# GpSimd's two-tensor operations in instructions of at most 256 columns

## The chip, the cores and the metric

The kernel runs on one core of a Trainium2 chip. Its engines take their instructions from queues of their own and meet at semaphores: TensorE (PE in the profile; PEld is its weight load), VectorE (DVE), ScalarE (ACT), GpSimd (POOL) and SyncE (SP), which here only issues transfers. The metric is the device time of one execution in microseconds, as the median of several runs.

## The reference

A decoder trunk of two layers over 16 + 1024 = 1040 tokens of width 1024, in float32. Layer 0 is a Mamba-2 mixer (SSD) with a convolutional gated FFN, layer 1 stick-breaking attention with the same FFN:

```python
h = concatenate([meta_tokens, x])
# layer 0
z, xbc, dt = split(rmsnorm(h) @ w_in); xbc = silu(dwconv4(xbc))
y = ssd(xbc, dt)                     # 32 heads of 64, 4 groups, state 128
h = h + (rmsnorm_by_group(y * silu(z)) * gate_g) @ w_out
h = h + ffn(rmsnorm(h))
# layer 1
k, v = split(rmsnorm(h) @ w_kv); q = rmsnorm(h) @ w_q
h = h + stick_breaking(q, k, v) @ w_o          # 16 heads of 64
h = h + ffn(rmsnorm(h))
out = rmsnorm(h)[16:]
# ffn(u): g, val = split(dwconv3(u @ w_up)); (silu(g) * val) @ w_down,  FF = 2816
```

## The kernel before

**Split operands.** Tokens lie along the free dimension in tiles of up to 348 columns, features in 128 partitions. A float32 operand of a matrix product is held as two tiles of type fp32r, a rounded part and the rest: ScalarE copies `w32` into `wh`, GpSimd (for most weights) or VectorE computes `wl = w32 - wh`, and `mm3` (lines 171 to 173) issues three matmuls, wh·uh, wh·ul and wl·uh. A weight tile has 1024 columns (768 or 512 in the output projections).

**Stages, in the order of time.** Read `x` and build the normed operands (to about 110 us); the SSD mixer (to 690), where `stream` runs the input projection's tiles between the chunks of 116 tokens; the output projection and the entry into the FFN (to 955); the up projection (to 1350); the down projection (to 1550); attention (to 2160); its output projection and the FFN's entry (to 2330); up (to 2740), down (to 2925) and the last norm.

**GpSimd's work on two tensors.** The rests of weights: `load_w` line 165 (with a scaling by a gain at line 162 for three uses), `up_weights` line 905 and `operands` line 1055, `weights` line 1114, and lines 1212 and 1217 for the first head pair. In the up projection also the sums and differences of halves of weight tiles, each 512 columns (lines 909 to 913). In the SSD stage, for every chunk: `ce` times the C matrix in `ssd_decays` (line 602; 8 heads by 116 columns), `xde` in `ssd_front` (line 631; 8 by 64) and the decayed `state` in `ssd_back` (line 650; 8 by 64). At the end a gain on 512 columns (line 1491). GpSimd also runs masks, memsets and sums of squares (`square_sum`, `parts` of the norm, line 321), which have at most 348 columns or are not touched.

**VectorE's work beside it.** The chunk's decays `dk` (line 598, eight instructions for a chunk), the gate norm (lines 209 to 212 and 545), splits into high and low parts (lines 190, 857, 1057), convolutions (line 296, one input in PSUM or in a copy `ft`), the gate product (line 947), sums of tiles in the up projection (line 955), the down projection's sums of operands (lines 1039 to 1050) and of products from PSUM (lines 403 and 1105).

**FFN.** Up and down use a seven-product scheme on halves of the operands. A block `b` of the up projection needs the weights f1 to f4, made by `up_weights` one block ahead: f1, f2 and f3 of 1024 columns, f4 of 512. The buffers `fh`/`fl` are two of each, `wh`/`wl` three. In the down projection every product takes an operand pair from `operands(i)`: differences on VectorE, `wh` and `gh` on ScalarE, `wl` on GpSimd, `gl` on VectorE.

**Order.** In the SSD stage and in attention (`manual_schedule`) PE, DVE, ACT and POOL run in the order of the code. Elsewhere the framework's planner orders each engine's instructions by its own estimate of costs when the program is built; a few edges (`behind`) pin single instructions. An instruction waits for the pieces of a tile that it reads, and engines serve their queues in order. GpSimd's queue also issues a few transfers (`spill`, line 382).

Of the kernel before, what the change touches and what calls it, by code (L numbers as in the profile page):

```python
# [8 lines left out]
F32 = mybir.dt.float32  # L9
F32R = mybir.dt.float32r  # L10
AF = mybir.ActivationFunctionType
ALU = mybir.AluOpType
# [57 lines left out]
ORD = ((0, 0), (1, 0), (0, 1), (1, 1), (0, 2), (1, 2))  # L70
XB, SQD = 9, (1, 4, 7)
SCALE = 0.125


_PAR = {}
_n = 0
for _name, _w in (
# [4 lines left out]
    _PAR[_name] = (_n, _w)  # L82
    _n += _w
NPAR = _n


class Trunk:
# [67 lines left out]
    def load_w(self, src, n, gain=None, out=None):  # L155
        nc = self.nc
        w32 = self.wp.tile([P, 1024], F32, tag="w32", name=self.nm("w32"))
        nc.sync.dma_start(w32[:, :n], src)
        if gain is not None:
            v = w32[:, :n].rearrange("p (k c) -> p k c", k=KD)  # L160
            g = gain.unsqueeze(2).to_broadcast([P, KD, n // KD])
            nc.gpsimd.tensor_tensor(v, v, g, op=ALU.mult)
        wh, wl = out or [self.wp.tile([P, 1024], F32R, tag=t, name=self.nm(t)) for t in ("wh", "wl")]
        nc.scalar.activation(wh[:, :n], w32[:, :n], AF.Copy)  # L164
        nc.gpsimd.tensor_tensor(wl[:, :n], w32[:, :n], wh[:, :n].bitcast(F32), op=ALU.subtract)  # L165
        return wh, wl

    def mm3(self, out, wh, wl, uh, ul, first, last, joins=False):
# [410 lines left out]
    def ssd_decays(self, g, ct, c, pool):  # L579

        nc = self.nc
        h0 = GH * g
        t0, n = CH[c]
        cc = 3 * (c % 3) + c // 3
        dk = pool.tile([P, 1024], F32, tag="D", name=self.nm("D"))
        dk = dk[:n, : GH * CB].rearrange("p (h l) -> p h l", h=GH)
        nc.sync.dma_start(dk, self.acs_d[c, h0 : h0 + GH].unsqueeze(0).to_broadcast([n, GH, CB]))
        dk = dk[:, :, :n]
        ce = None
        if c:  # L590
            ce = pool.tile([P, GH * CB], F32, tag="E", name=self.nm("E"), bufs=2)
            ce = ce.rearrange("p (h l) -> p h l", h=GH)
            nc.sync.dma_start(ce, self.ea_d[c, h0 : h0 + GH].unsqueeze(0).to_broadcast([P, GH, CB]))
            ce = ce[:, :, :n]
        yield dk, ce

        for i in range(GH):
            nc.vector.tensor_scalar(dk[:, i], dk[:, i], self.cols[:n, 1, cc, h0 + i : h0 + i + 1], 0.0, op0=ALU.subtract, op1=ALU.min)  # L598
        nc.scalar.activation(dk, dk, AF.Exp)
        yield  # L600
        if c:
            nc.gpsimd.tensor_tensor(ce, ce, ct[:, t0 : t0 + n].unsqueeze(1).to_broadcast([P, GH, n]), op=ALU.mult)
        yield

    def ssd_front(self, g, x, bt, ct, c, dk, pool):

        nc = self.nc
        h0 = GH * g
        tt = nc.vector.tensor_tensor
        t0, n = CH[c]  # L610
        cc = 3 * (c % 3) + c // 3
        e = t0 + n
        pcb = self.sm("cb")
        nc.tensor.matmul(pcb[:n, :n], bt[:, t0:e], ct[:, t0:e], start=True, stop=True)
        px = self.lg("px")
        for q in range(4):
            nc.tensor.transpose(px[:n, q * P : q * P + P], x[q][:, t0:e], self.ident)
        px = px[:n].rearrange("p (h d) -> p h d", h=GH)
        cbm = pool.tile([P, CB], F32, tag="cbm", name=self.nm("cbm"), bufs=2)
        tt(cbm[:n, :n], pcb[:n, :n], self.past[:n, :n], op=ALU.mult)  # L620
        xdt = pool.tile([P, GH, 64], F32, tag="xdt", name=self.nm("xdt"), bufs=2)
        tt(xdt[:n], px, self.cols[:n, 0, cc, h0 : h0 + GH].unsqueeze(2).to_broadcast([n, GH, 64]), op=ALU.mult)
        tt(dk, dk, cbm[:n, :n].unsqueeze(1).to_broadcast([n, GH, n]), op=ALU.mult)
        bk = xde = None
        if c < 8:
            pb = self.sm("pb")
            nc.tensor.transpose(pb[:n, :P], bt[:, t0:e], self.ident)
            bk = pool.tile([P, P], F32, tag="bk", name=self.nm("bk"), bufs=2)
            nc.scalar.activation(bk[:n], pb[:n, :P], AF.Copy)  # L629
            xde = pool.tile([P, GH, 64], F32, tag="xde", name=self.nm("xde"), bufs=2)  # L630
            nc.gpsimd.tensor_tensor(xde[:n], xdt[:n], self.cols[:n, 2, cc, h0 : h0 + GH].unsqueeze(2).to_broadcast([n, GH, 64]), op=ALU.mult)
        return xdt, xde, bk

    def ssd_back(self, g, x, c, dk, ce, xdt, xde, bk, state, pool):

        nc = self.nc
        h0 = GH * g
        t0, n = CH[c]
        cc = 3 * (c % 3) + c // 3
        e = t0 + n  # L640
        new = None
        if c < 8:
            ps = self.lg("S")
            nc.tensor.matmul(ps, bk[:n], xde[:n].rearrange("p h d -> p (h d)"), start=True, stop=True)
            new = pool.tile([P, GH, 64], F32, tag="state", name=self.nm("state"), bufs=2)
            psv = ps.rearrange("p (h d) -> p h d", h=GH)
            if c == 0:
                nc.scalar.activation(new, psv, AF.Copy)
            else:
                nc.gpsimd.tensor_tensor(new, state, self.cd[:, cc, h0 : h0 + GH].unsqueeze(2).to_broadcast([P, GH, 64]), op=ALU.mult)  # L650
                nc.vector.tensor_tensor(new, new, psv, op=ALU.add)
        py = self.sm("y")
        for i in range(GH):
            q, r = i // 2, 64 * (i % 2)
            y = py[r : r + 64, q * CB : q * CB + n]
            nc.tensor.matmul(y, xdt[:n, i, :], dk[:, i, :], start=True, stop=c == 0)
            if c:
                nc.tensor.matmul(y, state[:, i, :], ce[:, i, :], start=False, stop=True)
        for q in range(4):
            nc.vector.scalar_tensor_tensor(x[q][:, t0:e], x[q][:, t0:e], self.par("d_skip", 4 * g + q),  # L660
                                           py[:, q * CB : q * CB + n], op0=ALU.mult, op1=ALU.add)
        return new
# [227 lines left out]
    def up_weights(self, layer, b, pool):  # L890


        nc, a = self.nc, self.a
        H = D // 2
        tt = nc.gpsimd.tensor_tensor
        g, v = (self.wp.tile([P, 1024], F32, tag="w32", name=self.nm("w32")) for _ in range(2))
        nc.sync.dma_start(g, a["w_up"][layer, b])
        nc.sync.dma_start(v, a["w_up"][layer, KF + b])
        x, y = (pool.tile([P, QW], F32, tag="x32", name=self.nm("x32"), bufs=2) for _ in range(2))

        def parts(t, n, own):
            p, tags = (pool, ("fh", "fl")) if own else (self.wp, ("wh", "wl"))
            hi, lo = (p.tile([P, 1024], F32R, tag=tag, name=self.nm(tag)) for tag in tags)
            nc.scalar.activation(hi[:, :n], t, AF.Copy)  # L904
            tt(lo[:, :n], t, hi[:, :n].bitcast(F32), op=ALU.subtract)  # L905
            return hi, lo

        f1 = parts(g, D, False)
        tt(x[:, :H], v[:, :H], v[:, H:], op=ALU.add)
        tt(x[:, H:D], x[:, :H], g[:, :H], op=ALU.subtract)  # L910
        f2 = parts(x[:, :D], D, True)
        tt(y[:, :H], g[:, :H], v[:, :H], op=ALU.subtract)
        tt(y[:, H:D], g[:, H:], x[:, H:D], op=ALU.subtract)
        f3 = parts(y[:, :D], D, True)
        yield [(*f1, 0), (*f1, H), (*f2, H), (*f2, 0), (*f3, 0), (*f3, H)]
        f4 = parts(v[:, H:], H, False)
        yield [(*f4, 0)]
# [75 lines left out]
    def down(self, layer, gd, hd, pool, after, each=None):  # L993
# [4 lines left out]
        FN, S, H = FFN[layer].tile, FFN[layer].half, D // 2  # L998
        wide = FFN[layer].wide
        tt = nc.vector.tensor_tensor  # L1000
        pt = nc.gpsimd.tensor_tensor
        ADD, SUB = ALU.add, ALU.subtract
        half = lambda j: slice(S - S * j, 2 * S - S * j)

# [185 lines left out]
    def heads(self, u, p, pool):  # L1190
# [4 lines left out]
        class Pair:  # L1195
# [4 lines left out]
            def load(me, kind):  # L1200
# [8 lines left out]

                def scale():  # L1210
                    v = w32.rearrange("p (k c) -> p k c", k=KD)
                    nc.gpsimd.tensor_tensor(v, v, self.par(gain, 0, KD).unsqueeze(2).to_broadcast([P, KD, P]), op=ALU.mult)

                def parts():
                    me.w[kind] = wh, wl = [self.wp.tile([P, 1024], F32R, tag=t, name=self.nm(t)) for t in ("wh", "wl")]
                    nc.scalar.activation(wh, w32, AF.Copy)
                    nc.gpsimd.tensor_tensor(wl, w32, wh.bitcast(F32), op=ALU.subtract)

                def some(k0):

# [250 lines left out]
    def finish_tokens(self, h, chunks):  # L1471
# [10 lines left out]
        for i, (t0, m) in enumerate(chunks):  # L1482
            y = self.Q("y")[:, :D]
            for b in range(2):
# [3 lines left out]
                    nc.tensor.transpose(p[:m, k * P : k * P + P], h[4 * b + k][:, t0 : t0 + m], self.ident)  # L1488
                if b:
                    nc.scalar.activation(y[:m, w], p[:m], AF.Copy, scale=r[:m, i : i + 1])  # L1490
                    nc.gpsimd.tensor_tensor(y[:m, w], y[:m, w], self.gfin[:m, w], op=ALU.mult)
                else:
                    nc.vector.scalar_tensor_tensor(y[:m, w], p[:m], r[:m, i : i + 1], self.gfin[:m, w], op0=ALU.mult, op1=ALU.mult)
            nc.sync.dma_start(self.a["out"][t0 : t0 + m, :], y)
# [138 lines left out]
```

## Time and profile before

| | |
|---|---|
| runs shown, median (lowest to highest) | 2992.21 us (2991.93 to 2997.83) |
| profiled execution: time / span from first to last instruction | 2995.8 / 2994.1 us |
| mean granted TensorE clock | 0.983 |
| TENSOR_TENSOR instructions on GpSimd | 621 |

The profile is of one execution. Times in it are microseconds from the first instruction. A row of the timeline reads: start, duration, engine, line, operation, output<-inputs, shape, count, and in brackets how long the engine was idle before it and what ended that. A group row gives busy time and mean nanoseconds of one; a row of one line's instructions gives least, median and longest nanoseconds. "Busy" counts an instruction from its start to its end, waiting for a port included. Matmuls overlap, so their rows last longer than their distance.

### The profile page before, as it was taken

What the parts mean: (1) busy time and instruction counts of PE and PEld (TensorE: products, weight loads), DVE (VectorE), ACT (ScalarE), POOL (GpSimd) and SP (SyncE); (2) the same over time, 40 slices, a digit from 0 to 9 for tenths busy, and PEclk for the clock granted to TensorE, in tenths of its full rate; (3) what the DMA queues carried; (4) which work ended last, traced back from release to release, by engine and by line L of the source; (5) the groups of instructions that cost most, each with busy time, mean ns of one, the idle gap of its engine ahead of it and who ended that gap; (6) DMA issues with size and microseconds to landing.
All of it is one profiled execution on the core that took longest, in us unless ns stands there. A gap on an engine that the chain in (4) does not pass through costs nothing.

```text
span 2994.1 us, 57318 instructions
## 1 busy us (share of the span) xinstructions
PE 2879.0 (96%) x21863; PEld 2738.0 (91%) x21863; DVE 2304.0 (77%) x4026; ACT 1653.4 (55%) x3403; POOL 1308.0 (44%) x1250
## 2 busy tenths in 40 slices
PE   7999999989998999999999999999899999999998
PEld 4999898879998999998999999999798999998878
DVE  5586868885369887878876888888839878878785
ACT  4555555553245555555334788887736555554433
POOL 1254444442334666663442222222342766764451
PEclk9999999999999999999999999999999999999999
DMA  5233333323122222224232122221331222225321
GB/s 162 70 107 90 106 89 105 106 70 139 63 80 72 79 73 84 79 86 177 74 130 86 55 61 66 64 70 54 106 141 57 80 84 78 75 82 176 106 99 64
DMA packets 123411, 272.72 MB, mean 91 GB/s; under 512 B 13664, under 2 KB 53216, under 8 KB 123136
## 3 DMA queue, kind: packets, MB, share of 16 engines
q1 hardware_dynamic: 117760, 257.93, 26.6%
q10 hardware_dynamic: 4112, 6.56, 0.7%
q0 software_dynamic: 1264, 4.57, 0.4%
q8 instruction: 172, 2.82, 0.4%
q14 instruction: 103, 0.84, 0.1%
HBM read 200.89 MB, written 53.20 MB: 85 GB/s over the span
## 4 chain that ended last, share of the span: by engine, by line
PE 77%; DVE 12%; issue 4%; ACT 3%; POOL 2%; DMA 2%; SPq 0%; DVEq 0%; ACTq 0%; POOLq 0%
PE p L172 9%; PE p L171 9%; PE p L173 9%; PE acc L172 6%; PE acc L171 6%; PE acc L173 6%; PE pj L171 6%; PE pj L172 6%; PE pj L173 6%; PE po L1366 3%; PE lg L1325 3%; PE wT L1352 2%; DVE D L598 1%; PE ms L831 1%; DVE xbc L545 1%
## 5 line engine op out<-in xcount | busy, mean ns | idle before, releaser
L171 PE MATMUL pj<-uh,wh 128*128 128x348 f32 (+2 forms) x1536 | 507.0, 330 | 11.7 <-ACT bk L629 5.9
L172 PE MATMUL pj<-ul,wh 128*128 128x348 f32 (+2 forms) x1536 | 499.7, 325 | 0.0
L173 PE MATMUL pj<-uh,wl 128*128 128x348 f32 (+2 forms) x1536 | 496.3, 323 | 0.0
L171 PE MATMUL p<-bh,fh 128*128 128x262 f32 (+1 forms) x1408 | 403.5, 287 | 7.7 <-ACT c L293 2.8
L173 PE MATMUL p<-bh,fl 128*128 128x262 f32 (+1 forms) x1408 | 402.6, 286 | 3.6 <-POOL fl L905 3.6
L172 PE MATMUL p<-bl,fh 128*128 128x262 f32 (+1 forms) x1408 | 402.3, 286 | 0.1
L905 POOL TENSOR_TENSOR fl<-x,fh 128x1024 fp32r<-128x1024 f32 x88 | 212.4, 2414 | 267.4 <-ACT fh L904 217.7
L172 PE MATMUL p<-bl,wh 128*128 128x262 f32 (+1 forms) x1056 | 302.0, 286 | 6.1 <-DVE bl L857 6.1
L171 PEld LDWEIGHTS pj<-uh,wh 128*128 128x128 f32 x1536 | 292.8, 191 | 16.2 <-ACT xbc L293 4.3
L171 PE MATMUL p<-bh,wh 128*128 128x262 f32 (+1 forms) x1056 | 302.8, 287 | 0.9 <-ACT bh L856 0.9
L173 PE MATMUL p<-bh,wl 128*128 128x262 f32 (+1 forms) x1056 | 301.9, 286 | 0.0
L165 POOL TENSOR_TENSOR wl<-w,wh 128x1024 fp32r<-128x1024 f32 (+2 forms) x76 | 155.7, 2050 | 318.7 <-ACT wh L164 318.7
L172 PEld LDWEIGHTS pj<-ul,wh 128*128 128x128 f32 x1536 | 293.2, 191 | 1.8 <-issue 1.0
L173 PEld LDWEIGHTS pj<-uh,wl 128*128 128x128 f32 x1536 | 292.7, 191 | 0.8 <-issue 0.8
L296 DVE SCALAR_TENSOR_TENSOR c<-p,params,c 128x260 f32<-128x260 f32 (+1 forms) x528 | 249.8, 481 | 54.6 <-ACT c L293 45.1
L171 PEld LDWEIGHTS p<-bh,fh 128*128 128x128 f32 x1408 | 270.2, 192 | 8.6 <-ACT c L293 6.0
L173 PEld LDWEIGHTS p<-bh,fl 128*128 128x128 f32 x1408 | 269.4, 192 | 4.1 <-POOL fl L905 4.0
L172 PEld LDWEIGHTS p<-bl,fh 128*128 128x128 f32 x1408 | 270.2, 192 | 0.6 <-DVE bl L857 0.5
L947 DVE TENSOR_TENSOR c<-c,c 128x260 f32<-128x260 f32 (+1 forms) x176 | 245.0, 1394 | 5.5 <-ACT c L943 2.4
L952 ACT ACTIVATE ft<-p 128x262 f32<-128x262 f32 (+1 forms) x352 | 127.4, 384 | 203.8 <-DVE p L955 177.0
L1055 POOL TENSOR_TENSOR wl<-w,wh 128x1024 fp32r<-128x1024 f32 x56 | 148.9, 2662 | 205.4 <-ACT wh L1054 195.7
L171 PE MATMUL acc<-gh,wh 128*128 128x260 f32 (+1 forms) x672 | 215.0, 323 | 10.9 <-DVE h L1105 7.2
(325 smaller groups left out, 8472.7 us busy)
## 6 DMA issues: line engine op xcount, KB each, us to landing
w<-in_w_up SPq DMA_DIRECT2D x88, 512.0 KB
w<-in_w_down SPq DMA_DIRECT2D x44, 512.0 KB
w<-in_w_in SPq DMA_DIRECT2D x40, 512.0 KB
E<-ea_d SPq DMA_DIRECT2D x32, 464.0 KB
D<-acs_d SPq DMA_DIRECT2D x32, 420.5 KB
g<-c SPq DMA_DIRECT2D x88, 130.0 KB
g<-c SPq DMA_DIRECT2D x88, 128.0 KB
b<-g SPq DMA_DIRECT2D x16, 520.0 KB
```

The source lines that it names most:

```text
L165: nc.gpsimd.tensor_tensor(wl[:, :n], w32[:, :n], wh[:, :n].bitcast(F32), op=ALU.subtract)
L171: mm(out, wh, uh, start=first, stop=False, skip_group_check=joins)
L172: mm(out, wh, ul, start=False, stop=False, skip_group_check=joins)
L173: mm(out, wl, uh, start=False, stop=last, skip_group_check=joins)
L296: nc.vector.scalar_tensor_tensor(out, ps[:, o + i : o + i + n], wcol(i), out, op0=ALU.mult, op1=ALU.add)
L905: tt(lo[:, :n], t, hi[:, :n].bitcast(F32), op=ALU.subtract)
L947: self.last_up = tt(g[:, :FN], g[:, :FN], v[:, :FN], op=ALU.mult)
L952: nc.scalar.activation(s[:, :N], ps[:, :N], AF.Copy)
L1055: pt(wl, y, wh.bitcast(F32), op=SUB)
L1325: nc.tensor.matmul(ps[:nt, :m], part[:, c0 : c0 + nt], ks[a][:, s0 : s0 + m], start=x == 0, stop=x == 1)
L1352: nc.tensor.transpose(pt[:ns, x * CB : x * CB + nt], bt[a][:nt, x * CB : x * CB + ns], self.ident[:nt, :nt])
L1366: nc.tensor.matmul(po[64 * a : 64 * a + 64, :nt], v[: CH[c][1], c, 64 * a : 64 * a + 64], wt[a][: CH[c][1], c, :nt], start=x == 0, stop=x ...
```

## The change

Every `tensor_tensor` of GpSimd with more than 256 columns is issued as several instructions, each over at most 256 columns (for three-dimensional operands as many whole rows of the first free dimension as fit: two of 116 or 128 columns, four of 64). A new function does it, and the calls go through it. Operands, results and the order of the calls stay as they are; the other engines' code is not touched.

```diff
+PIECE = 256
...
+def pieces(eng, out, x, y, op):
+
+    n = out.shape[1]
+    size = 1
+    for d in out.shape[2:]:
+        size *= d
+    step = max(1, PIECE // size)
+    for a in range(0, n, step):
+        c = slice(a, min(a + step, n))
+        eng.tensor_tensor(out[:, c], x[:, c], y[:, c], op=op)
...
-        nc.gpsimd.tensor_tensor(wl[:, :n], w32[:, :n], wh[:, :n].bitcast(F32), op=ALU.subtract)
+        pieces(nc.gpsimd, wl[:, :n], w32[:, :n], wh[:, :n].bitcast(F32), ALU.subtract)
...
-            nc.gpsimd.tensor_tensor(ce, ce, ct[:, t0 : t0 + n].unsqueeze(1).to_broadcast([P, GH, n]), op=ALU.mult)
+            pieces(nc.gpsimd, ce, ce, ct[:, t0 : t0 + n].unsqueeze(1).to_broadcast([P, GH, n]), ALU.mult)
...
-                nc.gpsimd.tensor_tensor(new, state, self.cd[:, cc, h0 : h0 + GH].unsqueeze(2).to_broadcast([P, GH, 64]), op=ALU.mult)
+                pieces(nc.gpsimd, new, state, self.cd[:, cc, h0 : h0 + GH].unsqueeze(2).to_broadcast([P, GH, 64]), ALU.mult)
...
-        tt = nc.gpsimd.tensor_tensor
+        tt = lambda out, x, y, op: pieces(nc.gpsimd, out, x, y, op)
...
-        pt = nc.gpsimd.tensor_tensor
+        pt = lambda out, x, y, op: pieces(nc.gpsimd, out, x, y, op)
```

The same replacement is made for the scaling in `load_w`, for `xde`, at lines 1212, 1217 and 1491. Below the new function a line of the changed kernel has a number higher by 13.

More of the change, by code (lines that the diff above doesn't have):

```diff
@@ L161, in load_w @@
             g = gain.unsqueeze(2).to_broadcast([P, KD, n // KD])
-            nc.gpsimd.tensor_tensor(v, v, g, op=ALU.mult)
+            pieces(nc.gpsimd, v, v, g, ALU.mult)
         wh, wl = out or [self.wp.tile([P, 1024], F32R, tag=t, name=self.nm(t)) for t in ("wh", "wl")]
         nc.scalar.activation(wh[:, :n], w32[:, :n], AF.Copy)
-        nc.gpsimd.tensor_tensor(wl[:, :n], w32[:, :n], wh[:, :n].bitcast(F32), op=ALU.subtract)
+        pieces(nc.gpsimd, wl[:, :n], w32[:, :n], wh[:, :n].bitcast(F32), ALU.subtract)
         return wh, wl
@@ L630, in ssd_front @@
             xde = pool.tile([P, GH, 64], F32, tag="xde", name=self.nm("xde"), bufs=2)
-            nc.gpsimd.tensor_tensor(xde[:n], xdt[:n], self.cols[:n, 2, cc, h0 : h0 + GH].unsqueeze(2).to_broadcast([n, GH, 64]), op=ALU.mult)
+            pieces(nc.gpsimd, xde[:n], xdt[:n], self.cols[:n, 2, cc, h0 : h0 + GH].unsqueeze(2).to_broadcast([n, GH, 64]), ALU.mult)
         return xdt, xde, bk
@@ L1211, in scale @@
                     v = w32.rearrange("p (k c) -> p k c", k=KD)
-                    nc.gpsimd.tensor_tensor(v, v, self.par(gain, 0, KD).unsqueeze(2).to_broadcast([P, KD, P]), op=ALU.mult)
+                    pieces(nc.gpsimd, v, v, self.par(gain, 0, KD).unsqueeze(2).to_broadcast([P, KD, P]), ALU.mult)
                 def parts():
@@ L1216, in parts @@
                     nc.scalar.activation(wh, w32, AF.Copy)
-                    nc.gpsimd.tensor_tensor(wl, w32, wh.bitcast(F32), op=ALU.subtract)
+                    pieces(nc.gpsimd, wl, w32, wh.bitcast(F32), ALU.subtract)
                 def some(k0):
@@ L1490, in finish_tokens @@
                     nc.scalar.activation(y[:m, w], p[:m], AF.Copy, scale=r[:m, i : i + 1])
-                    nc.gpsimd.tensor_tensor(y[:m, w], y[:m, w], self.gfin[:m, w], op=ALU.mult)
+                    pieces(nc.gpsimd, y[:m, w], y[:m, w], self.gfin[:m, w], ALU.mult)
                 else:
```

## The prediction

> **What bounds the kernel now.** First the page's busy shares and its chain of waits, then the table by stage (from and to, length, busy time of PE, PEld, DVE, ACT and POOL with instructions, granted clock, DMA), to see where TensorE is not fed.
>
> ```profile
> PE 2879.0 (96%) x21863; PEld 2738.0 (91%) x21863; DVE 2304.0 (77%) x4026; ACT 1653.4 (55%) x3403; POOL 1308.0 (44%) x1250
> ...
> PE 77%; DVE 12%; issue 4%; ACT 3%; POOL 2%; DMA 2%; SPq 0%; DVEq 0%; ACTq 0%; POOLq 0%
> ```
>
> ```profile
> 110.00:690.00 580.00, 552.01 (x3998) 515.22 (x3997) 443.04 (x910) 302.70 (x434) 256.10 (x137) 0.97 0.32 94
> ...
> 975.00:1350.00 375.00, 375.00 (x3081) 375.00 (x3081) 300.88 (x479) 217.69 (x439) 250.30 (x144) 1.00 0.25 83
> 1350.00:1570.00 220.00, 205.76 (x1684) 204.36 (x1683) 181.89 (x216) 90.05 (x127) 89.91 (x36) 0.98 0.36 124
> ...
> 2735.00:2930.00 195.00, 184.05 (x864) 151.97 (x863) 167.17 (x152) 76.36 (x93) 90.34 (x35) 0.97 0.30 104
> ```
>
> TensorE bounds it. In the up projection (975 to 1350) it is busy 375.00 of 375: nothing done to GpSimd or VectorE can win time there. What can be won lies in the joints between stages, where TensorE waits: 14.2 us in one down projection (220 - 205.76), 11.0 in the other, 28.0 in the SSD stage. So I asked the timeline for the waits of TensorE and for what stood before them.
>
> ```profile
> 843.92 0.39 PE L171 MATMUL acc<-y,w 128*128 128x260 f32 x1 [3.44 <-DVE h L403]
> 957.04 0.36 PE L171 MATMUL p<-bh,fh 128*128 128x262 f32 x1 [2.80 <-DVE c L296]
> 2332.47 0.36 PE L171 MATMUL p<-bh,fh 128*128 128x258 f32 x1 [2.83 <-ACT c L293]
> 1370.81 0.35 PE L171 MATMUL acc<-gh,wh 128*128 128x260 f32 x1 [1.36 <-DVE c L296]
> 1394.15 0.56 PE L171 MATMUL acc<-gh,wh 128*128 128x260 f32 x1 [4.95 <-DVE h L1105]
> 1484.00 0.39 PE L171 MATMUL acc<-gh,wh 128*128 128x260 f32 x1 [1.62 <-DVE h L1105]
> 1498.55 0.38 PE L171 MATMUL acc<-gh,wh 128*128 128x260 f32 x1 [2.31 <-DVE p L1105]
> 2758.39 0.80 PE L172 MATMUL acc<-gl,wh 128*128 128x512 f32 x1 [5.13 <-DVE gl L1057]
> 2890.00 0.50 PE L173 MATMUL acc<-gh,wl 128*128 128x512 f32 x1 [1.74 <-POOL wl L1055]
> ```
>
> Eight of these nine waits (24.4 us together) end on VectorE or on what follows it. Why VectorE is late, the following rows show:
>
> ```profile
> 943.78 2.41 POOL L905 TENSOR_TENSOR fl<-x,fh 128x1024 fp32r<-128x1024 f32 x1
> 943.85 2.63 DVE L955 TENSOR_TENSOR ft<-ft,ft 128x262 f32<-128x262 f32 x1
> 946.14 1.49 POOL L905 TENSOR_TENSOR wl<-w,wh 128x512 fp32r<-128x512 f32 x1
> 947.15 0.76 DVE L296 SCALAR_TENSOR_TENSOR c<-ft,params,c 128x260 f32<-128x260 f32 x1 [0.68 <-ACT c L293]
> 947.59 1.47 POOL L909 TENSOR_TENSOR x<-w 128x512 f32<-128x512 f32 x1
> 947.84 1.51 DVE L955 TENSOR_TENSOR ft<-ft,ft 128x262 f32<-128x262 f32 x1
> ```
>
> ```profile
> L947 DVE TENSOR_TENSOR c<-c,c x176: 411/1350/2601, 932.5 to 2742.2; 128x260 f32<-128x260 f32 x88, 128x256 f32<-128x256 f32 x88
> L1057 DVE TENSOR_TENSOR gl<-b,gh x56: 1209/1234/3446, 1351.5 to 2875.7; 128x1040 fp32r<-128x1040 f32 x28, 128x1024 fp32r<-128x1024 f32 x28
> ```
>
> L947 takes 0.41 us alone and 1.35 in the median: a VectorE instruction whose two inputs lie in SBUF runs only when GpSimd's two-tensor instruction has ended. L955 of 943.85 ends at 946.48, 0.3 after L905 (946.19). And the two take turns: GpSimd's next instruction is already issued at 946.14, yet VectorE comes in between, and GpSimd's takes 1.49 where its kind needs 1.29. So at each end of a GpSimd instruction the waiting VectorE instruction is let in, and no sooner.
>
> **The change part by part.** Nothing is computed otherwise; some 600 instructions become some 1,800.
>
> *What a piece costs.*
>
> ```profile
> 2945.11 1.54 POOL L245 TENSOR_TENSOR sq<-sq,sq 128x256 f32<-128x256 f32 x2 [17.41 <-ACT sq L239]
> 2949.47 0.73 POOL L245 TENSOR_TENSOR sq<-sq,sq 128x256 f32<-128x256 f32 x1 [2.81 <-ACT sq L239]
> ...
> 1066.62 2.39 POOL L905 TENSOR_TENSOR fl<-x,fh 128x1024 fp32r<-128x1024 f32 x1 [3.67 <-ACT fh L904]
> ...
> 1070.27 1.29 POOL L909 TENSOR_TENSOR x<-w 128x512 f32<-128x512 f32 x1
> ```
>
> 256 columns take 0.73 us. An instruction starts 0.04 before the one ahead ends (946.14 + 1.49 against 947.59, above), so pieces follow at 0.69: four take 3 x 0.69 + 0.73 = 2.80 against 2.39, +0.41 for 1024 columns; two take 1.42 against 1.29, +0.13 for 512. With about 255 of the first size, 32 of 928 columns priced like them and 310 of 512, GpSimd's own time grows by 287 x 0.41 + 310 x 0.13 = 158 us, to about 1,470. Bounds for a piece: 0.60 (a quarter of 2.39) and 0.73 plus the 0.08 that L245's pair of 1.54 shows between two dependent instructions, 0.81.
>
> The Trainium skill speaks against the change here: GPSIMD Engine Reference, section 2.1, says that every instruction is broadcast and then looked up in software, tens of cycles each. By that an estimate for 1,200 more instructions, at 50 cycles of its 1.2 GHz, is 50 us more of GpSimd's time; the row of 0.73 shows three times that, and the sum below would be the same by both, as long as the up projection hides it.
>
> *Up projection.* One block is 7 products of 12 matmuls for two tiles, 168 x 375/3081 = 20.4 us, with three instructions of 1024 (two `fl`, one `wl`) and five of 512 (`wl` of f4, L909, L910, L912, L913). They grow by 3 x 0.41 + 5 x 0.13 = 1.9, from 250.30/375 x 20.4 = 13.6 to 15.5. Let each of the ten VectorE instructions of a block that read two SBUF tensors (four L947, two L955, four L296 on `ft`) take its turn at 0.3, what is left of 0.41 once it is let in: 18.5. That still fits into 20.4, TensorE's time covers it: 0. If that cover is gone, each block is late by the excess.
>
> *VectorE's waits at the joints.* A blocked instruction now waits for one piece, 0.6 us at most for the part that holds it up, not up to 2.2.
>
> ```profile
> L190 DVE TENSOR_TENSOR y<-xbc,y x8: 687/1243/2831, 787.6 to 840.7; 128x520 fp32r<-128x520 f32 x8
> ```
>
> ```profile
> 835.54 2.42 DVE L190 TENSOR_TENSOR y<-xbc,y 128x520 fp32r<-128x520 f32 x2 [0.71 <-ACT y L189]
> ...
> 838.30 5.23 DVE L190 TENSOR_TENSOR y<-xbc,y 128x520 fp32r<-128x520 f32 x2
> ...
> 951.51 2.65 DVE L296 SCALAR_TENSOR_TENSOR c<-ft,params,c 128x260 f32<-128x260 f32 x1
> ...
> 2743.69 3.43 DVE L1040 TENSOR_TENSOR b<-b,b 128x1024 f32<-128x1024 f32 x1
> ```
>
> Before 843.92: a free L190 takes 0.69, a pair that follows at 0.6 some 1.30, so the second pair lost 3.93; at 0.6 each it loses 1.2. I take 2.7 of the 3.44. Before 957.04: L955 2.2, L955 1.1 and L296 2.17 lost, 5.5 in all, now 3 x 0.6: 3.7 saved, more than the wait; I take 2.4 of 2.80, and the same 2.4 for its twin at 2332.47. In the down projections long VectorE instructions of 1.23 stand in a row, and each piece left over blocks the next one, so most of the loss comes back in smaller parts: a 1024-column instruction that cost them 2.2 costs up to 4 x 0.6 = 2.4 while the row lasts. There I take 2.0 of 4.95 and 2.0 of 5.13 (bounds 0 and the whole), since the row ends in additions from PSUM (L1105) that wait for nobody. At 1370.81, 1484.00 and 1498.55 one blocked instruction stands just ahead of such an end: 1.0, 1.2 and 1.6. Together 15.3 us, between 5 and 24.4.
>
> *The clock.*
>
> ```profile
> 958.30:961.70 3.40, 3.40 (x18) 3.40 (x17) 3.28 (x7) 0.39 (x2) 0.75 (x1) 0.50 0.23 78
> 1391.80:1398.60 6.80, 4.45 (x20) 4.48 (x21) 6.80 (x9) 0.39 (x1) 0.79 (x1) 0.50 0.01 2
> ```
>
> Behind 957.04 the granted clock is 0.50 for 3.4 us, behind 1394.15 for 6.8; a wait that vanishes gives back half of that. I take 1.7 each for 957.04 and its twin, 3.4; none for the others (bounds 0 and 10).
>
> *First pieces.* At 2890.00 TensorE waits for a whole L1055; its first matmuls need the first 256 columns alone. I take 1.0 (bounds: -1.7 and +0.4, if it waits for all four).
>
> *What it costs.* In the SSD stage the order of GpSimd, VectorE, ScalarE and TensorE is that of the code, and 28 us of waits lie open.
>
> ```profile
> 337.78 0.63 PE L171 MATMUL pj<-uh,wh 128*128 128x352 f32 x1 [3.01 <-ACT bk L629]
> 298.93 1.60 DVE L598 TENSOR_SCALAR D<-D,cols 116x116 f32<-116x116 f32 x8
> ...
> 330.21 4.04 DVE L598 TENSOR_SCALAR D<-D,cols 116x116 f32<-116x116 f32 x8
> ...
> 329.62 2.21 POOL L602 TENSOR_TENSOR E<-E,xbc 128x928 f32<-128x928 f32 x1
> 331.77 1.05 POOL L650 TENSOR_TENSOR state<-state,cd 128x512 f32<-128x512 f32 x1
> ```
>
> Eight short L598 in a row are free at 298.93 (1.60) and meet L602 and L650 at 330.21 (4.04, so 2.4 lost). Every one of the five pieces still to come blocks the next of them, 5 x 0.6 = 3.0: +0.6. For some six such places, two at each end of a group: +3.6 (bounds -3 and +10, since single VectorE instructions ahead of them gain). L650's `new`, on which L651 waits, and L631's `xde`, on which L644 waits, come 0.15 later each, L602 and L165 0.41: VectorE is busy 443 of 580 here and takes most of it. With attention's first weights (L1212, L1217): +1.5.
>
> Sum: -15.3 - 3.4 - 1.0 + 3.6 + 1.5 = -14.6 us. The profiled execution took 2995.8 (span 2994.1), 3.6 above the median of the runs; 2995.8 - 14.6 = 2981.2, on the runs' scale 2992.2 - 14.6 = 2977.6.
>
> **Rivals.** *GpSimd becomes the bound in the up projection (slower).* It decides from (20.4 - 3.0)/22 = 0.79 us a piece. At the upper bound 0.81 each of some 42 blocks is 0.4 late; at 0.85, 1.3, or +55 - 15: 3032. The 0.73 speaks against it; that it is the price of an addition in place, not of `fl`, speaks for it. Chance 0.07.
>
> *No turn between pieces (slower):* GpSimd's next piece goes ahead of the waiting VectorE. Then a blocked instruction loses 2.8, not 2.2, at about 14 open places: +8, and +4 in the SSD stage: 3004. The row at 946.14 speaks against it. The Trainium skill (SBUF — State Buffer, "Who interferes with whom") says that the pair of ports is held for a whole instruction and that issue order decides; it does not say who comes next. Chance 0.08.
>
> *GpSimd falls behind long VectorE rows (no change).* If each piece yields to an instruction of 1.23, a `wl` takes 4 x (0.6 + 1.2) = 7.2 us where a product lasts 5.8 (48 matmuls at 375/3081 = 0.12); TensorE then waits for GpSimd instead, 1.4 at some ten products, and the 14.6 is gone: 2992. So too if the planner's order outside the two hand-ordered stages comes out worse. Chance 0.20.
>
> *All waits of the table and their dips vanish:* 24.4 + 10 - 5: 2963. Chance 0.11.
>
> **How the numbers follow.** The forecast (2970 to 2985) has 0.54. A measurement here tells 0.2%, 6 us, from no change: faster 0.54 + 0.11 = 0.65, within 0.17, slower 0.18 (the two slower rivals and a part of the third). The range reaches from 2958 (past the last rival) to 3003, which leaves out the larger half of the slower ones.
>
> **What would show it.** Right: 256-column instructions at 0.70 to 0.75 us; L947's median under 0.8; the waits at 843.92, 957.04 and 2332.47 under 1.0 with a clock of 1.00 behind them; POOL busy above 1,450 with the up stages still at full TensorE. Wrong: L947 still at 1.3 (no turns), new TensorE waits for `wl` or `fl`, or waits in the SSD stage grown by more than 10.

## The result, and the profile after it

The changed kernel takes 2966.02 us (median of 4 runs, 2962.1 to 2966.99) beside 2992.07 (2991.28 to 2997.83) before: the ratio is 0.9905, 95% interval 0.9893 to 0.9917. That is 26.1 us less; 14.6 were forecast. The profiled execution took 2966.99, its span is 2965.3, mean clock 0.989.

Busy times, chain of waits and GpSimd's costliest group, from the page after; then the rows of one line's instructions (least/median/longest ns) for the gate product (L947, now L960) and the sum of two copies (L955, now L968); then the stage table for the same matmuls of the up projection and for the SSD stage:

```profile
PE 2870.4 (97%) x21863; PEld 2730.3 (92%) x21863; DVE 2139.3 (72%) x4026; ACT 1649.1 (56%) x3399; POOL 1614.5 (54%) x2434
...
PE 81%; DVE 9%; issue 3%; ACT 2%; POOL 2%; DMA 2%; SPq 0%; DVEq 0%; ACTq 0%; POOLq 0%
...
L97 POOL TENSOR_TENSOR wl<-w,wh 128x256 fp32r<-128x256 f32 x780 | 692.1, 917 | 459.0 <-ACT wh L177 294.2
```

```profile
L960 DVE TENSOR_TENSOR c<-c,c x176: 414/566/962, 920.3 to 2715.8; 128x260 f32<-128x260 f32 x88, 128x256 f32<-128x256 f32 x88
...
L968 DVE TENSOR_TENSOR ft<-ft,ft x88: 419/773/6500, 903.3 to 2707.0; 128x262 f32<-128x262 f32 x44, 128x258 f32<-128x258 f32 x44
```

```profile
961.60:1336.60 375.00, 375.00 (x3079) 375.00 (x3079) 254.88 (x480) 219.78 (x440) 303.25 (x399) 1.00 0.25 82
110.00:685.00 575.00, 547.26 (x3980) 509.37 (x3980) 433.16 (x909) 301.03 (x435) 304.01 (x397) 0.98 0.32 95
```

(Every piece is L97.) The gate product's median fell from 1.35 to 0.57 us and its longest from 2.60 to 0.96, VectorE is busy 165 us less, GpSimd 307 more, and the up projection still runs at full TensorE. But one line got worse: the longest L968 takes 6.50, where L955 never took more than 2.65. TensorE's waits after, at the joint of 116 and at those of the forecast (at 843.92, 1370.81, 1484.00 and 2890.00 none is left; those at 958.19 and 2323.83 are new):

```profile
112.42 0.40 PE L184 MATMUL pj<-uh,wh 128*128 128x352 f32 x1 [0.67 <-DVE xbc L309]
958.19 0.39 PE L184 MATMUL p<-bh,wh 128*128 128x262 f32 x1 [1.93 <-ACT ft L965]
1378.45 0.56 PE L184 MATMUL acc<-gh,wh 128*128 128x260 f32 x1 [5.27 <-DVE h L1118]
1478.26 0.39 PE L184 MATMUL acc<-gh,wh 128*128 128x260 f32 x1 [1.02 <-DVE p L1118]
2323.83 0.56 PE L184 MATMUL p<-bh,wh 128*128 128x258 f32 x1 [2.20 <-ACT ft L965]
2733.89 0.80 PE L185 MATMUL acc<-gl,wh 128*128 128x512 f32 x1 [3.69 <-DVE gl L1070]
```

To see where the time went, each matmul of one profile is paired with the same one of the other (by line and by order on its line); the table has the median shift of the starts (us, after less before) in a window of 30 us around a time of before, and what the stage ahead of it added. The last column is the forecast's step.

| up to (time before) | shift | of it here | forecast |
|---|---|---|---|
| 100: load, operands | -4.7 | -4.7 | none |
| 150: the joint at 116 | -9.5 | -4.8 | none |
| 690: SSD | -6.9 | +2.5 | +3.6 |
| 870: output projection, wait at 843.92 | -11.8 | -4.8 | -2.7 |
| 1000: entry into the FFN, 957.04 and its dip | -13.4 | -1.6 | -4.1 |
| 1345: up | -13.4 | 0.0 | 0 |
| 1560: down | -19.2 | -5.8 | -5.8 |
| 2100: attention | -20.1 | -0.9 | +1.5 |
| 2290: its output projection | -21.7 | -1.6 | none |
| 2400: entry, 2332.47 and its dip | -23.1 | -1.3 | -4.1 |
| 2730: up | -23.1 | 0.0 | 0 |
| end: down, last norm | -28.8 | -5.8 | -3.0 |

The profiled execution of before lies 3.7 above its median of 2992.07, that of after 1.0 above its own: -28.8 + 2.7 = -26.1, as the runs have it. A single stage of one profile scatters by some 3 us where a clock dip comes or stays away: two kernels that differ from before only ahead of 125 us stood 2.7 and 3.4 later at 870 than at 830.

### The profile page after: what moved, and what is told of

The parts are those of the page before. It is cut to its first block, busy times and chain, and to the rows that moved or that the text cites. A ratio compares the mean times of both kernels' runs of the same rounds, so it can differ in the third digit from the quotient of the medians.

```text
span 2965.3 us, 58614 instructions
## 1 busy us (share of the span) xinstructions
PE 2870.4 (97%) x21863; PEld 2730.3 (92%) x21863; DVE 2139.3 (72%) x4026; ACT 1649.1 (56%) x3399; POOL 1614.5 (54%) x2434
## 4 chain that ended last, share of the span: by engine, by line
PE 81%; DVE 9%; issue 3%; ACT 2%; POOL 2%; DMA 2%; SPq 0%; DVEq 0%; ACTq 0%; POOLq 0%
PE p L184 10%; PE p L185 10%; PE p L186 10%; PE acc L185 7%; PE acc L184 7%; PE acc L186 7%; PE pj L184 6%; PE pj L185 6%; PE pj L186 6%; PE po L1379 3%; PE lg L1338 2%; PE wT L1365 2%; POOL wl L97 1%; PE ms L844 1%; DVE D L611 1%
## 5 line engine op out<-in xcount | busy, mean ns | idle before, releaser
L97 POOL TENSOR_TENSOR wl<-w,wh 128x256 fp32r<-128x256 f32 x780 | 692.1, 917 | 459.0 <-ACT wh L177 294.2
L97 POOL TENSOR_TENSOR fl<-x,fh 128x256 fp32r<-128x256 f32 x352 | 260.8, 772 | 165.4 <-ACT fh L917 113.5
L965 ACT ACTIVATE ft<-p 128x262 f32<-128x262 f32 (+1 forms) x352 | 133.3, 382 | 180.3 <-DVE p L968 108.1
L185 PE MATMUL acc<-gl,wh 128*128 128x260 f32 (+1 forms) x672 | 216.1, 322 | 3.7 <-DVE gl L1070 3.7
L186 PE MATMUL acc<-gh,wl 128*128 128x260 f32 (+1 forms) x672 | 215.0, 321 | 0.0
```

What stands on the lines that cost most here:

```text
L97: eng.tensor_tensor(out[:, c], x[:, c], y[:, c], op=op)
L185: mm(out, wh, ul, start=False, stop=False, skip_group_check=joins)
L186: mm(out, wl, uh, start=False, stop=last, skip_group_check=joins)
L965: nc.scalar.activation(s[:, :N], ps[:, :N], AF.Copy)
```

## The experiments

The theories: **A**, the gain is VectorE's shorter waits at GpSimd's instruction ends; **B**, it is the planner's order, which came out anew; **C**, it is readers that start on the first piece of a result; and, once L968's 6.5 us were seen, **D**, pieces can also shut VectorE out. Ratios are to the kernel before on the same chip (its medians there: 2989.5 to 2993.9).

### B: SP's order (b_pin), and the order of the decays' path (b_dt)

The 4.8 us at 116 lie ahead of all FFN work. VectorE's copy of `rows` and SP's transfers, before, after:

```profile
104.48 0.51 DVE L467 COPY rows<-rows 96x348 f32<-96x348 f32 x1
...
91.89 11.67 SPq L158 DMA_DIRECT2D w<-in_w_in  x2
105.01 0.81 SPq L471 DMA_DIRECT2D acs_d<-rows  x2
...
108.91 0.42 SPq L471 DMA_DIRECT2D acs_d<-rows  x1
...
120.45 0.63 PE L171 MATMUL pj<-uh,wh 128*128 128x348 f32 x1 [4.03 <-DVE xbc L296]
```

```profile
99.90 0.52 DVE L480 COPY rows<-rows 96x348 f32<-96x348 f32 x1 [2.60 <-PE rows L478]
...
91.31 0.33 SPq L171 DMA_DIRECT2D w<-in_w_in  x1
100.44 1.29 SPq L484 DMA_DIRECT2D acs_d<-rows  x3
```

Two things differ. A weight load no longer stands ahead of `acs_d` on SP. And the planner has ordered the decays' path anew: the three transfers of `acs_d` leave in a row, the last of them 7 to 8 us earlier, where the copy and all else are 4.6 to 4.7 earlier only because of the load stage (its VectorE waits, below). No GpSimd instruction runs between 103.2 and 111.5 before. b_pin moves the load alone; b_dt changes when the decays' path is called, and the planner then moves the load too. Neither has a piece:

```diff
-        nc.sync.dma_start(w32[:, :n], src)
+        pin(self, nc.sync.dma_start(w32[:, :n], src))    # the 9th load: behind the last transfer of E
```

```diff
-                if n % 3 == 2:
+                if n % 2 == 1:
                     next(dt, None)
```

> The kernel before with one edit: the ninth weight load of the input projection keeps to its place in the code, behind the chunk's decay transfers on SP's queue, instead of ahead of the transfers of acs_d. The planner moved that load there by itself when the pieces came in. Theory A (all of the gain comes from VectorE's shorter waits for GpSimd): nothing changes, 2992 +- 1, and TensorE's wait of 4.0 at 116 us stays. Theory B (the 4.8 us won between 100 and 125 us are SP's order, which has nothing to do with the pieces): 2992.1 - 4.8 = 2987.3 (2986 to 2989), the wait at 116 under 1.5.

> The kernel before, no pieces; only the three steps of the decays' path (dt_path) are called after tiles 1, 3 and 5 of the first group and not after 2, 5 and 8. By that the planner puts the exponentials of cd, cols and ea of ScalarE next to each other and the transfers of acs_d ahead of the ninth weight load, as in the changed kernel. Theory B2 (the 4.8 us won between 100 and 150 us come from the order of the decays' path on ScalarE, VectorE and TensorE, which the planner chose anew, and not from the pieces): TensorE's wait of 4.0 at 116 us becomes less than 1.5, 2992 - 4.8 = 2987 (2985 to 2989). Theory A (shorter waits of VectorE win them): 2992 +- 1.

b_pin: 2991.31, ratio 0.9996 (0.9985 to 1.0008); the joint takes 0.9 more, not 4.8 less. SP had only waited there for what wasn't ready. b_dt: 2990.5, 0.9993 (0.9982 to 1.0003); the joint takes 4.5 less than before:

```profile
117.42 0.40 PE L184 MATMUL pj<-uh,wh 128*128 128x352 f32 x1 [1.78 <-DVE xbc L309]
```

So the place of the load is refuted as the cause, and the planner's order of the decays' path makes such 4.5 us in a profile with not one piece in the kernel. There 3.4 of them were lost again at 843.92; in the median of the runs 2.1 are left, with an interval that includes no change at all. The order is a side effect of the change: with pieces of 512 it came out as before up to 118 us, and nothing was won at 116.

The planner changed its order in other places too, and no run holds it there. Between 850 and 1400 us VectorE and ScalarE run in the order of before (TensorE moves some matmuls near 930 and 1371); there 4.4 us were won. Elsewhere, near 840, 1480 to 1550, 2317 and 2765 among others, single instructions changed places, and more did near 710 and from 2200 to 2280. So at these joints B is not excluded by an experiment; for A speak the shorter waits in VectorE's own rows.

### A and C: other sizes (p512, p128), the reverse order (rev), FFN alone (ffn_only)

```diff
-PIECE = 256
+PIECE = 512        # p512; 128 in p128
...
-    for a in range(0, n, step):
+    for a in reversed(range(0, n, step)):        # rev alone, with PIECE = 256
```

ffn_only uses `pieces` only in `up_weights`, `operands` and `weights`.

> PIECE = 512. SP's order at 100 us is then that of the kernel before. Theory A: only the instructions of 1024 and 928 columns are split, a blocked VectorE instruction waits for 1.3 at most and not for 2.4, so about half of the remaining gain of 26.1 - 4.8 = 21.3 us is seen: 2992 - 10 = 2982 (2978 to 2987); the longest gate product (c<-c,c, 2.60 before, 0.96 with 256) about 1.7. Theory B alone (the planner's order makes the whole gain): 2992 +- 2.

> PIECE = 128. From 1.25 and 0.694 us between the starts of pieces of 512 and 256 columns a piece of 128 takes 0.416. A block of the up projection has 44 of them, 18.3 us, and with ten turns of 0.3 21.3, where TensorE needs 20.4. Rival 'GpSimd becomes the bound': 0.9 late in each of some 42 blocks, +38 - 28 = 3002 (2990 to 3020), TensorE waits for fl or wl in the up stages. If GpSimd's turns hide in each other it stays under TensorE's time: 2960 to 2966, the longest gate product at about 0.8.

> The pieces in reverse order, last columns first: a reader of the first 256 columns waits for all pieces, and VectorE's turns stay as they are. Theory A: 2966 to 2970, only the 1 to 2 us at 2890 are lost. Theory C (readers that start on the first piece make most of the gain): 2980 or more.

> Pieces only in up_weights and in the down projection (operands, weights); weights of the input and output projections, the SSD stage, attention and the end as before. Theory A: the gain of the joints at 844, 957, 1371 to 1500, 2332, 2758 and 2890 stays, 3.8 + 0.8 + 5.8 + 2.5 + 2.6 + 2.8 = 18, less what the 3.1 us of the start are, and the 4.8 at 116 are missing too: 2992 - 17 = 2975 (2972 to 2979).

| | median us | ratio (95%) |
|---|---|---|
| rev | 2965.71 | 0.991 (0.9894 to 0.9925) |
| p512 | 2970.42 | 0.9927 (0.9911 to 0.9943) |
| ffn_only | 2973.92 | 0.9935 (0.9922 to 0.9948) |
| p128 | 3105.82 | 1.038 (1.0360 to 1.0399) |

rev is as fast as the change: C falls, first pieces are worth nothing that can be seen. ffn_only wins 18.7 of the 26.1, as A has it. p512 wins 22 of them, more than the 10 expected, without the 4.8 at 116. In the first down projection half the relief was as good as all of it (6.3 won against 5.8); from 2730 to the end it won 2.7 against 5.8, where kernels with pieces of 256 in the down projection range from 2.7 to 6.7. At 957 and 2332 it was better (3.8 and 3.6 won there, against 0.8 to 1.6 and 0.5 to 1.3 with 256; the smaller number is counted from 930 and from 2320). p128 is slower by 3.8%, far past its expectation. The stage table of its first up projection, what TensorE waits for (from 980 to 1380), and L968 in the whole kernel:

```profile
1000.00:1390.00 390.00, 359.55 (x2842) 356.44 (x2841) 290.12 (x440) 198.23 (x407) 330.74 (x755) 0.97 0.22 70
```

```profile
PE p L184 <- ACT ft L965: 26.6, 13, 3.4
PE p L184 <- DVE c L309: 5.9, 3, 3.7
```

```profile
L968 DVE TENSOR_TENSOR ft<-ft,ft x88: 411/548/7891, 932.2 to 2835.1; 128x262 f32<-128x262 f32 x44, 128x258 f32<-128x258 f32 x44
```

GpSimd is idle for 59 of 390 us and TensorE never waits for `wl` or `fl` there: not GpSimd's own time is the bound. TensorE waits for copies (L965) that need the buffers of an L968 which VectorE could not begin; 37 of the 88 waited through four pieces or more.

### D: who is shut out (up512, turns, p128_turns)

One such wait in the changed kernel, VectorE's rows and then GpSimd's:

```profile
950.00 1.01 DVE L309 SCALAR_TENSOR_TENSOR c<-p,params,c 128x260 f32<-128x260 f32 x2 [0.84 <-ACT c L306]
950.93 6.29 DVE L968 TENSOR_TENSOR ft<-ft,ft 128x262 f32<-128x262 f32 x1
```

```profile
949.98 2.81 POOL L97 TENSOR_TENSOR fl<-x,fh 128x256 fp32r<-128x256 f32 x4
952.77 1.42 POOL L97 TENSOR_TENSOR wl<-w,wh 128x256 fp32r<-128x256 f32 x2
954.15 1.41 POOL L97 TENSOR_TENSOR x<-w 128x256 f32<-128x256 f32 x2
955.53 1.41 POOL L97 TENSOR_TENSOR x<-x,w 128x256 f32<-128x256 f32 x2
960.85 1.43 POOL L97 TENSOR_TENSOR fl<-x,fh 128x256 fp32r<-128x256 f32 x2 [3.92 <-ACT fh L917]
```

L968 passes eight piece ends (951.4 to 956.3) without its turn and ends 0.29 after GpSimd ran dry at 956.94; TensorE's wait at 958.19 follows. Before, a VectorE instruction saw one whole GpSimd instruction go by at most. When this L968 came, GpSimd was in the twelfth piece since it had last let VectorE in; those that came after up to eleven got in at the next end. turns measures this by itself (no part of the trunk is computed, the output is zeros): m operations of VectorE on PSUM, then one sum from SBUF, beside GpSimd's pieces on end. up512 gives only `up_weights` pieces of 512:

```diff
-        tt = lambda out, x, y, op: pieces(nc.gpsimd, out, x, y, op)
+        tt = lambda out, x, y, op: pieces(nc.gpsimd, out, x, y, op, 512)
```

> No trunk: the output is zeros, the kernel measures turns alone. In each of 26 trials GpSimd runs 34 differences of 256 columns (56 of 128, 24 of 512) on end; VectorE first runs m operations with one input in PSUM, then one sum of 262 columns from SBUF. Theory D, counted in pieces: the sum waits for one piece at most where it comes before the 12th piece, and until GpSimd is done where it comes later, for each size (m above 18 for 256, above 10 for 128, above 32 for 512). Counted in time (8 us): m above 17 for each size. Theory A alone: one piece at most in every trial.

> The changed kernel, but up_weights in pieces of 512 columns. In the changed kernel two additions ft<-ft,ft (950.93 and 2316.37) waited 6.3 and 6.5 us while GpSimd ran eight more pieces, and the joints at 957 and 2332 gave back 0.8 and 0.5 where the kernel with 512 everywhere gave back 3.8 and 3.6. Theory D (after some twelve pieces of GpSimd on end without a turn of VectorE, VectorE isn't let in until GpSimd runs dry; twelve pieces of 512 don't come about here): no VectorE instruction waits longer than 1.6, both joints win 3 more, 2966 - 6 = 2960 (2957 to 2963). If the two waits were chance: 2966 +- 1.

VectorE in turns, the last trial let in and the first shut out, for 256, 128 and 512 columns:

```profile
146.80 0.98 DVE L42 TENSOR_TENSOR q<-q,r 128x262 f32<-128x262 f32 x1
...
171.69 13.57 DVE L42 TENSOR_TENSOR q<-q,r 128x262 f32<-128x262 f32 x1
...
333.93 0.61 DVE L42 TENSOR_TENSOR q<-q,r 128x262 f32<-128x262 f32 x1
...
358.75 15.72 DVE L42 TENSOR_TENSOR q<-q,r 128x262 f32<-128x262 f32 x1
...
551.75 1.54 DVE L42 TENSOR_TENSOR q<-q,r 128x262 f32<-128x262 f32 x1
...
583.81 12.88 DVE L42 TENSOR_TENSOR q<-q,r 128x262 f32<-128x262 f32 x1
```

The sum is let in while GpSimd's 14th piece runs (13th with 512) and shut out from the 15th (16th, 14th) on: with 256 and 512 until the trial's last piece is done, with 128 until 3 to 9 of the 56 pieces are left, after 20 to 37 piece ends. Counted in time these limits are 9, 6 and 16 us: pieces count, not time. That is theory D, with 13 or 14 in place of 12; a 1024-column instruction in four pieces reaches that number four times sooner. But one wait of the same run doesn't fit it, that of the four-column copy with which the first trial of 512 opens:

```profile
447.30 29.27 DVE L39 COPY d<-gone 128x4 f32<-128x4 f32 x1 [1.38 <-POOL gone L35]
```

It came while the trial's first piece ran, three pieces of the trial before behind VectorE's last turn, and waited through all 24; in the other trials this copy got in by the end of the first piece. GpSimd had not run dry between these two trials, as it had between the others.

up512: 2963.65, 0.9904 (0.9889 to 0.9918). Its longest L968 takes 1.6 us, and the two waits and dips are gone; stage rows of the changed kernel, then of up512, around 958:

```profile
955.00:962.00 7.00, 5.07 (x29) 4.85 (x28) 5.93 (x10) 4.11 (x9) 3.08 (x5) 0.76 0.24 75
```

```profile
955.00:962.00 7.00, 7.00 (x60) 7.00 (x59) 6.81 (x12) 4.45 (x9) 6.06 (x5) 1.00 0.11 38
```

From 930 to 1000 and from 2320 to 2400 its matmuls gain 3.7 and 4.6 where the change gains 0.8 and 0.5. To see what that is worth in the runs, the changed kernel itself (after_same), up512 again and up512 with whole `ce`, `xde` and `state` went side by side:

> The changed kernel once more, beside the two others of this group on the same chip: 2966 +- 2.

> up_weights in pieces of 512, all else in 256, beside the changed kernel. By the stages of the profile it is 5.4 faster than the changed kernel, 6.9 of it at 957 and 2332; 0 to 1.5 of that may be the chance of one profile. Theory D: 2966 - 5 = 2961 (2959 to 2964). If the two long waits cost nothing in most executions: 2966 +- 1.

> As the last, and in the SSD stage ce, xde and state whole, as before the change. From 150 to 690 us the kernels with pieces there lost 2.5, 0.9 and 0.3 and won 0.4 against the kernel before, those without won 0.3, 1.3 and 2.2. By my forecast's step (pieces cost 3.6 in the SSD stage): 2961 - 3 = 2958; if these differences are the scatter of one profile: 2961 +- 1.

after_same 2966.13 (2962.47 to 2969.83), up512_b 2962.87 (2961.45 to 2965.5), up512_no_ssd 2966.08 (2962.88 to 2969.15). up512 is the fastest version, 3 us under the change by the medians, though the runs of the two overlap; whole instructions in the SSD stage win nothing (from 150 to 690 us its profile loses 3.0 against before, that of up512_b wins 0.4), so what the pieces cost there isn't shown: it is below this scatter.

Last, added turns in p128: ten sums of four columns for a block and tile.

```diff
+        seen = pool.tile([P, 4], F32, tag="seen", name=self.nm("seen"), bufs=1)
+        turn_for = lambda s: tt(seen, s[:, :4], s[:, :4], op=ALU.add)
...
                 nc.scalar.activation(s[:, :N], ps[:, :N], AF.Copy)
+                turn_for(s)
...
+                turn_for(o)
```

> PIECE = 128 as in p128, and in the up projection VectorE adds four columns of each fresh copy (ft) and of each convolution (c) to themselves, 10 such sums for a block and tile, of no use but that they take turns with GpSimd. In p128 TensorE lost 38 and 32 us in the two up projections, while ft<-ft,ft waited for 5 to 8 us in nearly every block. Theory D (VectorE isn't let in after 13 or more pieces on end, whatever their size): with the turns taken in between no ft<-ft,ft waits longer than 1.5, and the two stages lose less than 10 together: 3106 - 65 = 3041 (3030 to 3055), faster by added work. Rival 'GpSimd becomes the bound' (44 pieces of 0.416 and the turns are longer than the block's 20.4 us): more turns make it worse, 3106 + 10 to + 40.

```profile
L995 DVE TENSOR_TENSOR seen<-ft x352: 144/317/9226, 916.9 to 2849.3; 128x4 f32<-128x4 f32 x176
L995 DVE TENSOR_TENSOR seen<-c x352: 144/388/10324, 923.1 to 2855.2; 128x4 f32<-128x4 f32 x176
```

3117.42, 1.0383 (1.0346 to 1.0421): no help. L968 itself is shut out three times now instead of 37, but the small sums are shut out in its place, for up to 10.3 us. In nearly all of these cases the sum ahead of it had ended only three to five pieces earlier, so D, with its count from VectorE's last turn, falls in this form. What the cases have in common is another count: 12 to 25 pieces since one was last stretched past 0.53 us, that is, since GpSimd itself had to wait; the four-column sums slip by without stretching any. That this is the cause is read from the rows, not tried; some fifteen sums of this kernel that had to wait were let in at 13 to 38 such pieces, and the copy of turns at 447.30 was shut out three pieces behind a stretched one (0.69 us). What decides who is shut out stays open.

## Why the prediction was right, and where its sum was short

**Sign, place and mechanism hold, the size does not.** VectorE's waits for GpSimd were the cause of most of the gain: ffn_only wins 18.7 us with the order of before up to 837 us, and rev excludes first pieces. The planner's order at the later joints is excluded by no run. The 2966.0 lies below the 2970 to 2985 of the forecast and near the 2963 of the rival *All waits of the table and their dips vanish*, but not by that rival: waits of 5.27 and 3.69 are left, and 9.5 us come from stretches that neither had in its sum. That it came so near is chance. The price of a piece was 0.73: in turns 340 pieces of 256 take 0.727 in the mean and start 0.683 apart. GpSimd's own time isn't the bound in the up projection even at 128, so *GpSimd becomes the bound* falls as a mechanism. From 690 on the forecast's steps in the table sum to -18.2; measured are -28.8 + 6.9 = -21.9.

**The step that failed is the start: it had no term.** I read TensorE's waits from 338 us on and never asked for those of the first 120. There lie 9.5 of the 14 us that the sum is short of its profile. Most of the first 4.7 is the mechanism itself, in the load stage, where the order is that of before up to 42 us and 3.6 arise between 30 and 40; VectorE's `x<-x,r`, before and after:

```profile
26.63 6.23 DVE L360 TENSOR_SCALAR x<-x,r 116x1024 f32<-116x1024 f32 x3 [0.37 <-PE xT L343]
```

```profile
26.35 3.46 DVE L373 TENSOR_SCALAR x<-x,r 116x1024 f32<-116x1024 f32 x3 [0.37 <-PE xT L356]
```

2.8 us are won in these three instructions alone, on the way to the first `pj`. The other 4.8 are put down to the planner's order (b_dt); the prediction had that as a part of its third rival and only as a loss.

**Mis-sized terms.** At 957.04 and 2332.47, -4.1 each: the waits themselves vanished, but a new one with a dip of its own came 17 us later (958.19, 2323.83; clock 0.76 over the 7 us of the row above), and -1.6 and -1.3 were left. What failed is the sentence that at each end of a GpSimd instruction the waiting one is let in: true in the up projection for up to eleven pieces, not for twelve. A row of the prediction already spoke against it: the first L598 of 330.21 came before the end of L602 at 331.83, and the whole of L650 (to 332.82) went by before it. So the rival *No turn between pieces* came true at three places of the changed kernel (950.93, 2316.37 and an L791 at 844.25) and, at 128, for 37 of 88 sums. The Trainium skill (SBUF — State Buffer, "Who interferes with whom") says that the pair is held for a whole instruction, which the row of 943.85 bears out. The Trainium skill says there too that issue order decides who blocks; the wait at 950.93 contradicts this, as eight pieces that started after L968 went ahead of it.

At 1394.15 I took 2.0 of 4.95 and 5.27 are left: none. VectorE's row of twelve long instructions ahead of it, 22.6 us before (1371.04 to 1393.59), is 23.0 after (1354.86 to 1377.89), as GpSimd's 23 pieces stand beside it all the way:

```profile
1371.20 1.75 DVE L1055 TENSOR_TENSOR w<-w,w 128x1024 f32<-128x1024 f32 x1 [2.72 <-POOL wl L97]
```

```profile
1351.25 29.68 POOL L97 TENSOR_TENSOR wl<-w,wh 128x256 fp32r<-128x256 f32 x23 [16.92 <-ACT wh L1067]
```

1.29 a piece where 0.68 is its own distance: each yields to a VectorE instruction, as the third rival has it, and what four waits of 2.2 cost before comes back in twelve of 0.5 and in 2.72 us in which VectorE stands idle for `wl`. The down projection still made its 5.8, from the joints at 1371, 1447 and 1478 to 1510. At 2758.39, 2.0 was forecast of 5.13, and 1.4 went; another 1.2 or so came from the clock behind it, which had been put at nothing (0.63 over the 8 us before, 0.82 after). *First pieces* (-1.0 at 2890) came to -2.0 there, but with rev as well, so not by first pieces. Attention's +1.5 was -0.9, and +3.6 for the SSD stage was +2.5 in this profile but isn't borne out by up512_no_ssd.

**The dispatch estimate.** From 0.683 and 1.224 us between the starts of 256 and 512 columns, an instruction costs 0.683 - 0.541 = 0.142 beside its columns, 168 us for the 1,184 more. GpSimd's busy time grew by 307: the rest, by difference, is waiting for VectorE. The Trainium skill's tens of cycles (GPSIMD Engine Reference, section 2.1), 50 us by the estimate, are a third of it; neither reached the path.

## What to carry to other kernels

In this kernel VectorE and GpSimd both work from SBUF, and the length of GpSimd's instructions set that of most of VectorE's waits. Halving the longest ones gave 22 of the 26 us, the next halving began to cost at two joints, and pieces of 128 lost 113 against the kernel before. Look for the runs of short GpSimd instructions on end that a split makes, above all just ahead of a joint, and for the longest rather than the median wait on the other side. And when an edit goes through a planner, compare the order of the instructions before crediting the edit: here a sixth of the profile's gain came with a new order that won as much at that joint in the unsplit kernel.

## What the runs showed of the hardware

VectorE's turn between GpSimd's instructions isn't guaranteed. In turns a sum that came when 13 to 15 of them had run on end, of 128, 256 or 512 columns, waited up to 15.7 us: with 256 and 512 until GpSimd was done, with 128 until 3 to 9 of 56 pieces were left. A copy that came three pieces after VectorE's last turn waited 29.27. The Trainium skill (GPSIMD Engine Reference, section 2.1) says that consecutive instructions don't hold its cores together, each going on when its own share is done. No run here shows whether the waits have to do with that.
